# Eight PSUM banks in one list, and a limit on how far ahead weights are split

## The chip, the cores and the metric

The kernel runs on one core of a Trainium2 chip, as one program in one launch. The metric is the device time of that launch in microseconds, from several executions of the same program. Five engines work side by side, each through its own instructions in order: TensorE (PE) multiplies matrices, VectorE (DVE) and ScalarE (ACT) do elementwise work and read the matmul results, GpSimd (POOL) does a few small things, and SyncE (SP) issues nearly all DMA transfers. Engines wait for each other by semaphores.

## What is computed

Two layers, each with three sub-layers on a residual stream x of 256 tokens by 1024 features; every sub-layer is normalised and then shifted, scaled and gated by nine vectors that come from a conditioning vector c ("ada").

```python
for l in range(DEPTH):                       # 2
    mod = c_act @ ada_w[l] + ada_b[l]        # ada_w[l]: 1024 x 9216
    sh1, sc1, g1, sh2, sc2, g2, sh3, sc3, g3 = jnp.split(mod, N_MOD, axis=-1)
    h = modulate(rms_norm(x, norm_ffn1[l]), sh1, sc1)
    x = x + 0.5 * g1[:, None, :] * swiglu(h, ffn1_w_in[l], ffn1_w_out[l])   # d_ff 2816
    h = modulate(rms_norm(x, norm_mix[l]), sh2, sc2)
    x = x + g2[:, None, :] * token_mix(h, cos, sin, mix_w_in[l], sgu_w[l], sgu_b[l], mix_w_out[l])
    h = modulate(rms_norm(x, norm_ffn2[l]), sh3, sc3)
    x = x + 0.5 * g3[:, None, :] * swiglu(h, ffn2_w_in[l], ffn2_w_out[l])
return rms_norm(x, final_norm)
```

`swiglu(h, w_in, w_out)` is `(silu(g) * u) @ w_out` with `g, u` the halves of `h @ w_in`. All data are float32.

## The kernel before

**Units and splits.** Weights come from HBM in units of 512 KB, each by one DMA into one of five `raw` buffers (`NRAW`). A unit is split into a rounded part `whi` (ACT, L445) and the rest `wlo` (DVE, L446), both float32r, and a product is three matmuls: hi by hi, lo by hi and hi by lo. There are `NB` = 11 pairs of `whi`/`wlo`; a pair is used again when the matmuls of its unit are done (`ring`, `release`). `seq` is the one list of all units in order of use, with the ada units woven in between (`weave`); an ada unit is no split but one multiply-add on DVE (L430) into `aacc`.

**What sets the order.** The order on each engine is the order in which the Python code writes the instructions (a manual schedule). After each piece of work on PE the loops call `pump`, which writes the next one or two splits of `seq`, with the ada steps ahead of them, as far as the ring of 11 lets it. So ACT and DVE have splits queued for units well ahead of PE, and whatever is written after them stands behind them in the same queue.

**The feed-forward sub-layers.** There are four, called A, B (layer 0) and C, D (layer 1) here. The tokens are two halves b of 128. The first 512 columns of the hidden layer are done with the activations stationary, half by half (`ffn_gen`). The other 2304 columns go through `joint_gen`, the weight-stationary part: five chunks, J1 to J4 of 8 units and J5 of 4. A chunk keeps four accumulators (J5 two), each one PSUM bank of 128 x 512, one per 128 columns; a unit is 24 matmuls of 128x256 (L658, L660, L662), six for each accumulator. After the chunk's last unit the code writes the **evacuation**: for each accumulator a Silu on ACT (L667) and a multiply on DVE (L668), which is the last reader of the bank, and for each pair a split into `aThi`/`aTlo` (L474, L475). Then come the `pump` of that unit and the next chunk. At the end `project` multiplies by `w_out` (22 units, both halves one after the other with a lag).

**PSUM before.** Two pools: `accp` with six buffers for accumulators, and `tpp` with two for transposes and for the column sums of the ada vectors (`tp_tile`, L365, L366, L714). A pool gives its buffers out in turn, so in the joint part a chunk of four gets the two buffers that the chunk before didn't have, and then the first two that it had: its third and fourth accumulator lie where the chunk before had its first and second.

Of the kernel before, what the change touches and what calls it, by code (L numbers as in the profile page):

```python
# [23 lines left out]
NB = 11  # L24
LAG = 6
# [71 lines left out]
def trunk(ctx, tc, x_in, c_in, pos_in, ada_w, ada_b, norm_ffn1, ffn1_w_in, ffn1_w_out,  # L97
# [11 lines left out]
    accp = ctx.enter_context(tc.tile_pool(name="accp", bufs=6, space=bass.MemoryType.PSUM))  # L109
    tpp = ctx.enter_context(tc.tile_pool(name="tpp", bufs=2, space=bass.MemoryType.PSUM))  # L110
# [34 lines left out]
    def rope_tables():  # L145
# [7 lines left out]
        ang = const.tile([P, 2, 8], F32, name="ang")  # L153
# [45 lines left out]
    hThi = const.tile([P, 2, KD, P], F32R, name="hThi")  # L199
    hTlo = const.tile([P, 2, KD, P], F32R, name="hTlo")  # L200
# [102 lines left out]
    def defer(n, fn):  # L303
        pend.append([n, fn])
# [54 lines left out]
    def ada_finish(e, hi, lo, slot):  # L359
        def run():  # L360
            t = e["vec"]
            for h in range(2):
# [4 lines left out]
                V.tensor_tensor(t[:, sl], ps, t[:, sl], op=ALU.add)  # L367
            vec[(e["l"], e["kind"], e["v"] // 3 + 1)] = t
# [35 lines left out]
    def pump(quota=2, force=False):  # L404
# [3 lines left out]
        while sp[0] < len(seq) and quota > 0:  # L408
# [47 lines left out]
    wcur = [0, 0]  # L456

# [49 lines left out]
    def norm_T(b, l, i, h):  # L507
# [4 lines left out]
        for q in range(4):  # L512
# [4 lines left out]
            else:  # L517
                V.tensor_scalar(y[:, k, :], ps[:, q * P:(q + 1) * P], A, B, op0=ALU.mult, op1=ALU.add)

# [38 lines left out]
    def project(b, pi, n, operand, hook):  # L558
# [3 lines left out]
        acc = [accp.tile([P, 512], F32, name="acc", tag="acc")[:, :sl.stop - sl.start] for sl in parts]  # L562
# [12 lines left out]
        for h, sl in enumerate(parts):  # L575
# [10 lines left out]
            update(b, l, i, acc[h], sl)  # L586
            if h == 0 and SQ_D and not final:
# [13 lines left out]
    def ffn_gen(b, pi, env):  # L601
        hi, lo = hT[b]
        f = 0
        for c0, w in chunks[:1]:
            kt = 1024 // w
            acc = [accp.tile([P, 512], F32, name="acc", tag="acc") for _ in range(2)]
            for k0 in range(0, KD, kt):
                for s in range(2):
# [8 lines left out]
                    if last:  # L617
                        def ev(acc=acc, f=f, w=w):
                            a = xm[b][:, 512:1024]
                            S.activation(a[:, :w], acc[0][:, :w], AF.Silu)  # L620
                            V.tensor_tensor(a[:, :w], a[:, :w], acc[1][:, :w], op=ALU.mult)

# [66 lines left out]
    tp_ev = {}  # L689

    def tp_tile():
# [4 lines left out]
        return tpp.tile([P, 512], F32, name="tp", tag="tp")  # L696

    def evac_later(n, fn, tiles=1):
        done = []

# [4 lines left out]
        for m in range(tp_n[0] - tiles, tp_n[0]):  # L705
            tp_ev[m] = run
# [10 lines left out]
    def sgu_prep(l, env):  # L717
# [6 lines left out]
        def fin():  # L724
            ps = transposes(lambda i: wr[:, i, :], 4)
            S.activation(wT.rearrange("p g t -> p (g t)"), ps, AF.Copy)
        env["sgu_fin"] = fin
# [8 lines left out]
    def mix_gen(b, pi, env):  # L736
# [14 lines left out]
        def evac_idx():  # L751
# [4 lines left out]
            copy(D_V2, vS[:, b, 512 - VX:512], acc[:, 0:VX])  # L756
            rope(t[:, 0:320], 5, b, pool)
# [456 lines left out]
```

## Time and profile before

| | |
|---|---|
| median of three runs | 1050.22 us (1048.61 to 1052.21) |
| the profiled execution, its own time | 1047.78 us |
| its span, first to last instruction | 1046.0 us |
| PE busy | 994.6 us, 95% of the span |
| DVE, ACT busy | 780.2 us (75%), 541.6 us (52%) |
| read from HBM | 251.27 MB, mean 241 GB/s |
| chain that ended last | PE 67%, DMA 12%, DVE 12%, ACT 5%, issue 3% |

The first line is what is compared; the profile is one execution, and its span is 1.8 us shorter than its time. "Busy" of PE counts the time in which a matmul was under way, at whichever clock was granted. In the page's slices PE shows its lower digits in slices 4, 6, 16, 23 and 25 of 40 (7 to 8 tenths), all of them in the joint parts of A, B and C, and the clock row shows an 8 or a 9 beside some of them. The joint parts stand at 56 to 180 us (A), 372 to 481 (B), 565 to 688 (C) and 878 to 977 (D).

### The profile page before, as it was taken

The page shows a single profiled execution, that of the slowest core. Times are in us where ns is not written, and L with a number is a line of the kernel's source. Part 1 is how long each engine was busy: PE and PEld are TensorE (multiplying, and loading weights), DVE is VectorE, ACT ScalarE, POOL GpSimd, SP SyncE. Part 2 cuts the span into 40 slices and gives each one's busy share as a digit, 9 for nine tenths or more (in the row PEclk, how much of TensorE's full clock was granted, in tenths as well). Part 3 has the DMA queues.
Part 4 walks back from the last instruction along what each step waited for, and adds up shares of the span by engine and source line. Part 5 has one row for each costly group of instructions (what it writes and reads, how often), then busy time and mean ns, then how long its engine had stood idle before and what let it go on. Part 6 is the DMA issues. An engine that isn't in the chain of part 4 may idle for free.

```text
span 1046.0 us, 16540 instructions
## 1 busy us (share of the span) xinstructions
PE 994.6 (95%) x6352; PEld 884.1 (85%) x6352; DVE 780.2 (75%) x1095; ACT 541.6 (52%) x832; POOL 21.6 (2%) x39
## 2 busy tenths in 40 slices
PE   6996989999999998999999798999999999999997
PEld 3696979888778898998888798988888888999986
DVE  4887877778898887877668778776778878566453
ACT  5565444446577744544455444443557857444331
POOL 4000000000000000000000000000000000000000
PEclk9998999999999999999999899999999999999999
DMA  9888888985765598886848988878564548776531
GB/s 332 304 288 299 290 304 284 321 296 188 221 201 167 162 326 298 315 301 239 283 141 282 340 290 303 282 259 276 152 186 137 153 140 291 233 237 213 183 134 41
DMA packets 109774, 253.40 MB, mean 242 GB/s; under 512 B 8498, under 2 KB 26980, under 8 KB 109696
## 3 DMA queue, kind: packets, MB, share of 16 engines
q1 hardware_dynamic: 108864, 251.20, 71.7%
q8 instruction: 50, 0.82, 0.3%
q0 software_dynamic: 544, 0.63, 0.2%
q10 hardware_dynamic: 288, 0.52, 0.1%
q14 instruction: 28, 0.23, 0.1%
HBM read 251.27 MB, written 1.05 MB: 241 GB/s over the span
## 4 chain that ended last, share of the span: by engine, by line
PE 67%; DMA 12%; DVE 12%; ACT 5%; issue 3%; SPq 1%; POOL 0%; POOLq 0%; ACTq 0%; DVEq 0%
PE acc L478 14%; PE acc L480 14%; PE acc L479 13%; DMA raw<-in_ffn_w_in_dram 9%; PE acc L658 7%; PE acc L660 7%; PE acc L662 7%; DVE wlo L446 5%; ACT whi L445 3%; DVE aacc L430 3%; PE tp L714 2%; DMA raw<-in_ada_w_dram 1%; DMA sraw<-in_ada_w_dram 1%; DVE xm L668 1%; PE acc L1015 1%
## 5 line engine op out<-in xcount | busy, mean ns | idle before, releaser
L446 DVE TENSOR_TENSOR wlo<-raw,whi 128x1024 fp32r<-128x1024 f32 (+1 forms) x328 | 395.2, 1216 | 166.3 <-ACT whi L445 160.7
L445 ACT ACTIVATE whi<-raw 128x1024 fp32r<-128x1024 f32 (+1 forms) x328 | 339.0, 1048 | 301.3 <-PE acc L480 99.2
L658 PE MATMUL acc<-hThi,whi 128*128 128x256 f32 x1152 | 327.2, 284 | 29.6 <-DVE xm L668 29.6
L660 PE MATMUL acc<-hTlo,whi 128*128 128x256 f32 x1152 | 324.3, 281 | 0.0
L662 PE MATMUL acc<-hThi,wlo 128*128 128x256 f32 x1152 | 324.2, 281 | 0.0
L658 PEld LDWEIGHTS acc<-hThi,whi 128*128 128x128 f32 x1152 | 221.1, 192 | 31.3 <-DVE xm L668 31.0
L662 PEld LDWEIGHTS acc<-hThi,wlo 128*128 128x128 f32 x1152 | 221.8, 193 | 0.0
L660 PEld LDWEIGHTS acc<-hTlo,whi 128*128 128x128 f32 x1152 | 220.9, 192 | 0.3
L478 PE MATMUL acc<-whi,hThi 128*128 128x512 f32 (+1 forms) x384 | 154.7, 403 | 1.2 <-ACT hThi L1048 1.0
L480 PE MATMUL acc<-whi,hTlo 128*128 128x512 f32 (+1 forms) x384 | 148.6, 387 | 0.1
L479 PE MATMUL acc<-wlo,hThi 128*128 128x512 f32 (+1 forms) x384 | 147.5, 384 | 0.0
L430 DVE SCALAR_TENSOR_TENSOR aacc<-raw,ccol,aacc 128x1024 f32<-128x1024 f32 x112 | 143.3, 1279 | 3.0 <-DMA raw<-in_ada_w_dram 2.8
L478 PE MATMUL acc<-whi,aThi 128*128 128x512 f32 (+1 forms) x374 | 141.9, 380 | 0.0
L479 PE MATMUL acc<-wlo,aThi 128*128 128x512 f32 (+1 forms) x374 | 141.2, 378 | 0.0
L480 PE MATMUL acc<-whi,aTlo 128*128 128x512 f32 (+1 forms) x374 | 141.0, 377 | 0.0
L478 PEld LDWEIGHTS acc<-whi,hThi 128*128 128x128 f32 x384 | 72.4, 188 | 18.2 <-issue 3.2
L480 PEld LDWEIGHTS acc<-whi,hTlo 128*128 128x128 f32 x384 | 72.2, 188 | 16.0 <-DVE hTlo L1050 1.0
L479 PEld LDWEIGHTS acc<-wlo,hThi 128*128 128x128 f32 x384 | 72.4, 188 | 13.2 <-issue 0.5
L480 PEld LDWEIGHTS acc<-whi,aTlo 128*128 128x128 f32 x374 | 70.3, 188 | 13.2
L478 PEld LDWEIGHTS acc<-whi,aThi 128*128 128x128 f32 x374 | 70.4, 188 | 12.8
L479 PEld LDWEIGHTS acc<-wlo,aThi 128*128 128x128 f32 x374 | 70.4, 188 | 12.5
L491 ACT ACTIVATE xm<-x 128x512 f32<-128x512 f32 (+1 forms) x29 | 17.9, 617 | 61.7 <-DVE x L529 56.6
(152 smaller groups left out, 683.6 us busy)
## 6 DMA issues: line engine op xcount, KB each, us to landing
raw<-in_ffn_w_in_dram SPq DMA_DIRECT2D x176, 512.0 KB, 5.0
raw<-in_ada_w_dram SPq DMA_DIRECT2D x128, 512.0 KB, 5.2
raw<-in_ffn_w_out_dram SPq DMA_DIRECT2D x88, 512.0 KB, 5.0
raw<-in_mix_w_in_dram SPq DMA_DIRECT2D x40, 512.0 KB, 4.3
sraw<-in_ada_w_dram SPq DMA_DIRECT2D x32, 256.0 KB, 6.6
raw<-in_mix_w_out_dram SPq DMA_DIRECT2D x16, 512.0 KB, 3.6
vec<-in_ada_b_dram SPq DMA_DIRECT2D x6, 512.0 KB, 7.1
raw<-in_mix_w_in_dram SPq DMA_DIRECT2D x8, 324.0 KB, 3.1
```

What stands on the lines that cost most here:

```text
L430: V.scalar_tensor_tensor(aacc, e["raw"], ccol[:, j:j + 1], aacc, op0=ALU.mult, op1=ALU.add)
L445: S.activation(hi[:, :n], src, AF.Copy)
L446: V.tensor_tensor(lo[:, :n], src, hi[:, :n].bitcast(F32), op=ALU.subtract)
L478: T.matmul(ps, ahi, whi, start=first, stop=False)
L479: T.matmul(ps, ahi, wlo, start=False, stop=False)
L480: T.matmul(ps, alo, whi, start=False, stop=last)
L491: S.activation(xm[b][:, sl], x[b][:, sl], AF.Square, accum_out=ss[:, c:c + 1])
L658: T.matmul(o, wh[:, kk, sl], ahi, start=first, stop=False, skip_group_check=True)
L660: T.matmul(o, wh[:, kk, sl], alo, start=False, stop=False, skip_group_check=True)
L662: T.matmul(o, wl[:, kk, sl], ahi, start=False, stop=k == KD - 1, skip_group_check=True)
L668: V.tensor_tensor(a, a, acc[j][:, 256:], op=ALU.mult)
L714: T.transpose(ps[:, i * P:(i + 1) * P], src(i), ident)
```

## The change

1. PSUM is no longer two pools. Eight tiles of one bank each make one list, `banks`; `take()` removes the first, `give()` puts a bank at the end when the code has written its last reader. Every accumulator and every transpose tile takes from it, so each gets the bank that has been free the longest in the order of the program.
2. `pump` stops at a weight unit when `lead[0]` units are split and not yet taken by `next_w(0)`. `lead[0]` is 8 (`LEADJ`) during `joint_gen` and 11 elsewhere. What stands behind that unit in `seq`, ada units too, is held with it.
3. The small tile `ang` is allocated at another place.

No instruction of work is added or taken away. SP issues the same transfers in the same order.

```diff
@@ -106,8 +107,14 @@
-    accp = ctx.enter_context(tc.tile_pool(name="accp", bufs=6, space=bass.MemoryType.PSUM))
-    tpp = ctx.enter_context(tc.tile_pool(name="tpp", bufs=2, space=bass.MemoryType.PSUM))
+    bankp = ctx.enter_context(tc.tile_pool(name="bankp", bufs=1, space=bass.MemoryType.PSUM))
+    banks = [bankp.tile([P, 512], F32, name=f"bank{i}") for i in range(8)]
+
+    def take():
+        return banks.pop(0)
+
+    def give(*ts):
+        banks.extend(ts)
...
@@ -414,6 +422,8 @@
             r = len(ring)
+            if e["k"] == "w" and not force and len(W) - wcur[0] >= lead[0]:
+                break
             if need and r >= NB and not ring[r - NB]:
...
@@ -640,7 +655,7 @@
-            acc = [accp.tile([P, 512], F32, name="acc", tag="acc") for _ in range(nj)]
+            acc = [take() for _ in range(nj)]
...
@@ -666,6 +681,7 @@
                             S.activation(a, acc[j][:, :256], AF.Silu)
                             V.tensor_tensor(a, a, acc[j][:, 256:], op=ALU.mult)
+                            give(acc[j])
...
     def tp_tile():
...
-        return tpp.tile([P, 512], F32, name="tp", tag="tp")
+        t = tp_bank[m] = take()
+        return t
...
             if kind == "f":
                 both(n - KF)
+                lead[0] = LEADJ
                 for q, _ in enumerate(joint_gen(env)):
...
+                lead[0] = NB
             both(n)
```

ACT at the end of chunk J1 of A. `whi` of `raw` is a split, `xm0` of an accumulator is a Silu, `aThi` the split of two of them. Before:

```order
L445 ACTIVATE whi_758<-raw_679 128x1024
L445 ACTIVATE whi_767<-raw_719 128x1024
L445 ACTIVATE whi_808<-raw_756 128x1024
L445 ACTIVATE whi_817<-raw_765 128x1024
L445 ACTIVATE whi_852<-raw_806 128x1024
L445 ACTIVATE whi_863<-raw_815 128x1024
L667 ACTIVATE xm0_102<-acc_555 128x256
L667 ACTIVATE xm0_102<-acc_556 128x256
L474 ACTIVATE aThi_553<-xm0_102 128x512
```

And now, from the split of the same unit (`whi_741` here) on:

```order
L455 ACTIVATE whi_741<-raw_663 128x1024
L455 ACTIVATE whi_782<-raw_703 128x1024
L455 ACTIVATE whi_817<-raw_739 128x1024
L682 ACTIVATE xm0_107<-bank7_85 128x256
L682 ACTIVATE xm0_107<-bank1_79 128x256
L485 ACTIVATE aThi_543<-xm0_107 128x512
L682 ACTIVATE xm0_107<-bank6_84 128x256
L682 ACTIVATE xm0_107<-bank2_80 128x256
```

The evacuation moved up past three splits: the last split ahead of it was that of the tenth unit after the chunk, and is now that of the seventh.

PE at the start of J2 of A, first matmul of each accumulator. J1 had `acc_555` to `acc_558` before (`acc_918` and `acc_919` are the buffers of 555 and 556), and has banks 7, 1, 6 and 2 now. Before:

```order
L658 MATMUL acc_558<-hThi_106,whi_638 128x256
...
L658 MATMUL acc_916<-hThi_106,whi_675 128x256
...
L658 MATMUL acc_917<-hThi_106,whi_675 128x256
...
L658 MATMUL acc_918<-hThi_106,whi_675 128x256
...
L658 MATMUL acc_919<-hThi_106,whi_675 128x256
```

And now:

```order
L673 MATMUL bank2_80<-hThi_111,whi_623 128x256
...
L673 MATMUL bank5_83<-hThi_111,whi_659 128x256
...
L673 MATMUL bank0_78<-hThi_111,whi_659 128x256
...
L673 MATMUL bank3_81<-hThi_111,whi_659 128x256
...
L673 MATMUL bank4_82<-hThi_111,whi_659 128x256
```

J2 now takes no bank of J1.

PE at the start of J3 of A, where J2 had banks 5, 0, 3 and 4. `whi_1015` is an ada vector, whose column sums (`ones`) take two banks. Now:

```order
L677 MATMUL bank4_82<-hThi_111,wlo_865 128x256
L372 MATMUL bank1_79<-whi_1015,ones_97 128x512
L373 MATMUL bank1_79<-wlo_1016,ones_97 128x512
L372 MATMUL bank6_84<-whi_1015,ones_97 128x512
L373 MATMUL bank6_84<-wlo_1016,ones_97 128x512
L673 MATMUL bank2_80<-hThi_111,whi_899 128x256
...
L673 MATMUL bank7_85<-hThi_111,whi_899 128x256
...
L673 MATMUL bank5_83<-hThi_111,whi_899 128x256
...
L673 MATMUL bank0_78<-hThi_111,whi_899 128x256
```

Before, the column sums stood two units earlier, inside J2:

```order
L365 MATMUL tp_1121<-whi_979,ones_92 128x512
L366 MATMUL tp_1121<-wlo_980,ones_92 128x512
L365 MATMUL tp_1125<-whi_979,ones_92 128x512
L366 MATMUL tp_1125<-wlo_980,ones_92 128x512
L658 MATMUL acc_916<-hThi_106,whi_808 128x256
```

The sums moved to the chunk's border, and hold banks 1 and 6 when J3 takes its four: the third and fourth of J3 are the first two of J2.

## Rows read from the trace of the kernel before

**Rows 1.** Page, costliest groups: busy, mean ns of one, idle before and its releaser.

```profile
L658 PE MATMUL acc<-hThi,whi 128*128 128x256 f32 x1152 | 327.2, 284 | 29.6 <-DVE xm L668 29.6
L662 PE MATMUL acc<-hThi,wlo 128*128 128x256 f32 x1152 | 324.2, 281 | 0.0
```

**Rows 2.** Timeline, end of J1 in A: start, us, engine, line, operation, [idle before].

```profile
78.62 1.06 ACT L445 ACTIVATE whi<-raw 128x1024 fp32r<-128x1024 f32 x1 [2.57 <-DMA raw<-in_ffn_w_in_dram]
...
87.63 1.06 ACT L445 ACTIVATE whi<-raw 128x1024 fp32r<-128x1024 f32 x1 [2.81 <-DMA raw<-in_ffn_w_in_dram]
88.60 0.64 ACT L667 ACTIVATE xm<-acc 128x256 f32<-128x256 f32 x2
...
89.86 0.75 DVE L668 TENSOR_TENSOR xm<-xm,acc 128x256 f32<-128x256 f32 x2
...
90.33 0.58 PE L658 MATMUL acc<-hThi,whi 128*128 128x256 f32 x1 [9.53 <-DVE xm L668]
...
93.23 1.04 ACT L445 ACTIVATE whi<-raw 128x1024 fp32r<-128x1024 f32 x1
```

**Rows 3.** Timeline, the other waits of PE over 1 us for L668.

```profile
144.30 0.58 PE L658 MATMUL acc<-hThi,whi 128*128 128x256 f32 x1 [5.05 <-DVE xm L668]
...
399.69 0.53 PE L658 MATMUL acc<-hThi,whi 128*128 128x256 f32 x1 [3.87 <-DVE xm L668]
...
598.97 0.58 PE L658 MATMUL acc<-hThi,whi 128*128 128x256 f32 x1 [6.57 <-DVE xm L668]
...
626.25 0.39 PE L658 MATMUL acc<-hThi,whi 128*128 128x256 f32 x1 [1.71 <-DVE xm L668]
...
652.42 0.58 PE L658 MATMUL acc<-hThi,whi 128*128 128x256 f32 x1 [2.63 <-DVE xm L668]
```

**Rows 4.** Stretches behind five waits: length, PE busy (count), granted clock, DMA share, GB/s.

```profile
90.30:96.00 5.70, 5.67 (x26) 0.50 0.87 309
144.30:147.20 2.90, 2.90 (x13) 0.50 0.93 344
399.70:403.20 3.50, 3.50 (x16) 0.51 0.55 167
599.00:604.60 5.60, 5.60 (x26) 0.50 0.52 188
652.40:655.80 3.40, 3.38 (x16) 0.50 0.36 141
```

**Rows 5.** Stretches: length, busy PE, PEld, DVE, ACT, POOL, granted clock, DMA share, GB/s.

```profile
878.00:977.00 99.00, 99.00 (x872) 98.90 (x871) 65.31 (x71) 49.39 (x66) 0.00 (x0) 1.00 0.73 236
...
56.00:225.00 169.00, 154.42 (x1104) 145.82 (x1103) 134.97 (x168) 78.56 (x99) 0.00 (x0) 0.96 0.88 307
...
565.00:730.00 165.00, 152.37 (x1092) 143.90 (x1091) 126.08 (x134) 70.51 (x86) 0.00 (x0) 0.96 0.85 295
...
575.00:600.00 25.00, 17.70 (x145) 17.49 (x145) 18.88 (x20) 11.37 (x14) 0.00 (x0) 0.89 0.97 342
200.00:225.00 25.00, 25.00 (x114) 20.70 (x113) 19.46 (x17) 9.60 (x10) 0.00 (x0) 1.00 0.95 335
```

**Rows 6.** Timeline in A: split of J3's seventh unit, and the ada step behind it.

```profile
106.27 1.06 ACT L445 ACTIVATE whi<-raw 128x1024 fp32r<-128x1024 f32 x1 [1.77 <-PE acc L660]
107.36 1.23 DVE L446 TENSOR_TENSOR wlo<-raw,whi 128x1024 fp32r<-128x1024 f32 x1
108.51 1.28 DVE L430 SCALAR_TENSOR_TENSOR aacc<-raw,ccol,aacc 128x1024 f32<-128x1024 f32 x1
```

**Rows 7.** Price of a split and of an ada step on DVE, and its waits for ACT.

```profile
L446 DVE TENSOR_TENSOR wlo<-raw,whi 128x1024 fp32r<-128x1024 f32 (+1 forms) x328 | 395.2, 1216 | 166.3 <-ACT whi L445 160.7
...
L430 DVE SCALAR_TENSOR_TENSOR aacc<-raw,ccol,aacc 128x1024 f32<-128x1024 f32 x112 | 143.3, 1279 | 3.0 <-DMA raw<-in_ada_w_dram 2.8
...
119.73 1.99 ACT L445 ACTIVATE whi<-raw 128x1024 fp32r<-128x1024 f32 x2
```

More of the change, by code (lines that the diff above doesn't have):

```diff
@@ L24 @@
 NB = 11
+LEADJ = 8
 LAG = 6
@@ L367, in run @@
                 V.tensor_tensor(t[:, sl], ps, t[:, sl], op=ALU.add)
+                give(ps)
             vec[(e["l"], e["kind"], e["v"] // 3 + 1)] = t
@@ L518, in norm_T @@
                 V.tensor_scalar(y[:, k, :], ps[:, q * P:(q + 1) * P], A, B, op0=ALU.mult, op1=ALU.add)
+        give(ps)
         def split():
@@ L561, in project @@
         parts = PARTS if final and b == 1 else HALF
-        acc = [accp.tile([P, 512], F32, name="acc", tag="acc")[:, :sl.stop - sl.start] for sl in parts]
+        bk = [take() for _ in parts]
+        acc = [t[:, :sl.stop - sl.start] for t, sl in zip(bk, parts)]
         def part(k, w, h):
@@ L586, in project @@
             update(b, l, i, acc[h], sl)
+            give(bk[h])
             if h == 0 and SQ_D and not final:
@@ L605, in ffn_gen @@
             kt = 1024 // w
-            acc = [accp.tile([P, 512], F32, name="acc", tag="acc") for _ in range(2)]
+            acc = [take() for _ in range(2)]
             for k0 in range(0, KD, kt):
@@ L689, in trunk @@
     tp_ev = {}
+    tp_bank = {}
     def tp_tile():
@@ L704, in run @@
                 fn()
-        for m in range(tp_n[0] - tiles, tp_n[0]):
+                give(*[tp_bank.pop(m) for m in mine])
+        for m in mine:
             tp_ev[m] = run
@@ L726, in fin @@
             S.activation(wT.rearrange("p g t -> p (g t)"), ps, AF.Copy)
+            give(ps)
         env["sgu_fin"] = fin
@@ L756, in evac_idx @@
             copy(D_V2, vS[:, b, 512 - VX:512], acc[:, 0:VX])
+            give(acc)
             rope(t[:, 0:320], 5, b, pool)
@@ L786, in relu @@
                 S.activation(rl[:, e::2, :nk], st["lg"][e][:, :, :nk], AF.Relu)
+                give(st["lgb"][e])
             st["rl"] = rl
@@ L816, in evac_qk @@
                 S.activation(t, st["acc_k"], AF.Copy)
+            give(st["acc_" + nm])
             rope(t, 8, b, pool)
@@ L887, in evac_v @@
             copy(D_V, vS[:, b, :512 - VX], st["acc_v"][:, :512 - VX])
+            give(st["acc_v"])
         def pv(g):
@@ L891, in pv @@
             if g == 0:
-                st["pv"] = accp.tile([P, 512], F32, name="acc", tag="acc")
+                st["pv"] = take()
             ps = st["pv"]
@@ L904, in evac_att @@
             split_T(st["pv"].rearrange("p (k t) -> p k t", k=4), nhi[:, 4:8, :], nlo[:, 4:8, :])
+            give(st["pv"])
         def evac_gelu(nm):
@@ L908, in evac_gelu @@
             S.activation(t, st["acc_" + nm], AF.Gelu)
+            give(st["acc_" + nm])
             st[nm] = t
@@ L912, in sgu_mm @@
             va = st["va"]
-            ps = accp.tile([P, 512], F32, name="acc", tag="acc")
+            ps = take()
             for g in range(4):
@@ L924, in sgu_out @@
                                        op0=ALU.add, op1=ALU.mult)
+            give(ps)
         def tr_a():
@@ L973, in mix_gen @@
         for nm, c0, w in MIX_CHUNKS:
-            acc = accp.tile([P, 512], F32, name="acc", tag="acc")
+            acc = take()
             for k0 in range(0, KD, 2):
@@ L1025, in start_acc @@
         n_sd[0] += KD // SJ
+        if g + 2 >= NG:
+            give(su["dps"][g % 2])
     def start_col(g):
@@ L1057, in start_x @@
             S.activation(su["xhT"][:, h * 4:h * 4 + 4, b, :], ps.rearrange("p (k t) -> p k t", k=4), AF.Copy)
+            give(ps)
     def load_cols(l):
@@ L1070, in col_T @@
         S.activation(cols[:, l, :], ps[:, :96], AF.Copy)
+        give(ps)
     rope_it = rope_tables()
@@ L1081, in start @@
         su["acc"] = aap.tile([P, D], F32, name="aacc", tag="aacc")
-        su["dps"] = [accp.tile([P, 512], F32, name="acc", tag="acc") for _ in range(2)]
+        su["dps"] = [take() for _ in range(2)]
         dma_fill()
```

15 lines of the change are left out of this document (12 added, 3 removed).

## The prediction

> **What bounds the kernel now.** I read the page's engine shares first (the table above): PE is busy 994.6 of 1046 us, so the kernel can only win where PE stands still or runs slowly. Then the costliest groups, for PE's idle time: nearly all of it in the joint parts stands before L658, 29.6 us, and is ended by DVE's multiply L668, the last reader of an accumulator; before L662, the first to need `wlo`, it is 0.0 [rows 1]. So in the joint parts PE waits for banks and never for weights.
>
> The timeline says why. J1 of A has ended and PE has started J2, when it reaches J2's third accumulator, which lies where J1 had its first. It stands there for 9.53 us, until 90.33 [rows 2], so from 80.80. J1's evacuation was ready to go, but its Silu stood on ACT behind the split of the tenth unit after the chunk, which itself waited 2.81 us for its transfer and began at 87.63; the Silus came at 88.60, the multiplies at 89.86 [rows 2]. The split three places earlier began at 78.62 [rows 2]. The other waits are 5.05 us in A, 3.87 in B, and 6.57, 1.71 and 2.63 in C [rows 3]: with the first, 29.4 of the 29.6 us. D has none.
>
> What a wait costs is more than its length: behind five of the six PE runs at a granted clock of 0.50 (1.2 instead of 2.4 GHz) for 5.7, 2.9, 3.5, 5.6 and 3.4 us, though busy all the time [rows 4]. Half of that, 10.5 us, is lost. Through all of D, where PE never stops, the clock is 1.00 [rows 5]. D also gives the pace: 872 matmuls in 99.00 us, 0.1135 us each, so 2.72 us for a unit of 24 and 21.8 us for a chunk of eight.
>
> **The change, part by part.**
>
> *Banks by longest free.* At the border J1 to J2 in A the new order gives J2 four banks that J1 didn't have, so the wait has nothing to wait for, and J1's evacuation has a whole chunk of 21.8 us. The waits removed: A 9.53 + 5.05 = 14.58, B 3.87, C 10.91, together 29.4 us. With them goes half of the slow stretches behind them: A (5.7 + 2.9)/2 = 4.3, B 1.75, C 4.5, together 10.5. At most, then: A 18.9, B 5.6, C 15.4, in sum 39.9 us.
>
> *What isn't removed.* J3 of A still takes two banks of J2, as its third and fourth accumulators, since the column sums hold two others. After J2's end PE has 12 matmuls (1.4 us) to do before it wants the first of them, and ahead of those four of twice the width, some 0.9 us by D's pace: 2.3 us of grace. J2 would now run from 79.4 (80.80 less those 1.4) to 101.2, so PE is there at 103.5. J2's Silu stands behind the split of J3's seventh unit, which began at 106.27, and waited 1.77 us of that for PE, which will now be earlier [rows 6]: from 104.5, then. After it come its `wlo` of 1.23 us and an ada step of 1.28 ahead of the multiply on DVE [rows 6], whose single cost is 0.75/2 = 0.38 [rows 2]. As timed now the bank is free at 109.8 + 0.4 = 110.2, and without the 1.77 at 108.4: a new wait of 6.7 or of 4.9 us. The lower bound is zero, if ACT gets there before J2 ends. As one evacuation no longer sits between those splits and the transfers have some room left, I take 4.4, near the upper rows. With half of a slow stretch like the 2.9 us that followed the 5.05 us wait [rows 4] it is 5.9 (bounds 0 to 8.2).
>
> B's last border has the same pattern, with the fourth accumulator only: 18 matmuls, 2.0 us, before it is wanted, so a wait shorter than the 3.87 there now is possible. I leave B at 5.6 and keep 2.6 for the range. The 1.71 us wait shows that a short one costs no clock.
>
> *The transposes of `aacc`* and the column sums move two to four units later, the same instructions on the same engines. Their readers are two to three units away, and I cost it at nothing; covered by that distance, the price without cover is one border wait of some 2 us.
>
> *The cap of eight.* Splits that stood ahead of the evacuation now stand behind it. It removes no work. In A the evacuation takes ACT from 88.60 to 93.23, 4.6 us [rows 2], and splits written behind it come that much later; their cover is the stock, 8 x 2.72 = 21.8 us of PE's work. I cost it at nothing while that holds, and its failing is the third rival.
>
> *Supply.* A faster PE wants its weights sooner. The DMA share is 0.88 over 56 to 225 us and 0.85 over 565 to 730, where the best stretches of 25 us show 0.95 and 0.97 [rows 5]. With 0.96 as the ceiling A's 169 us can shrink to 154.9, C's 165 to 146.1: gains up to 14.1 and 18.9. So 18.9 in A is more than the transfers allow, 18.9 - 5.9 = 13.0 is just within, and 15.4 in C is near it. In 575 to 600, where C's longest wait lies, the transfers are already at the ceiling [rows 5]. For this closeness I take 1.5 off each; this is a choice between 0 and what the first rival would take.
>
> Sum: A 18.9 - 5.9 - 1.5 = 11.5; B 5.6; C 15.4 - 1.5 = 13.9; together 31.0 us. The profiled execution took 1047.8, which makes 1016.8; the median of the runs shown is 2.4 higher, 1050.2, which makes 1019.2. I say 1018.
>
> The clock term stands on [rows 4]: slow stretches only behind waits of 2.6 us and more. The Trainium skill (TensorE: Matmul & The Clock Gate, "A second HAM failure mode: psum-queue depth-cycling") speaks against part of it: it tells of a kernel that cycled through PSUM banks and whose clock fell again and again from micro-idling between groups of matmuls. By that page the 10.5 us would stay and the new time would be about 1027. D in this trace cycles through its six buffers at a clock of 1.00, so the trace doesn't agree.
>
> **The rivals.**
>
> *Supply takes over (first rival).* PE loses the wait for the bank and soon waits for `whi` or `wlo` instead. For it: the split at 93.23 is that of the eleventh unit after J1, the one at 119.73 that of the eighteenth [rows 2, 7]: seven units (and one ada vector) in 26.5 us, while PE at full pace takes 19.0. DVE waits 160.7 us in all for `whi` [rows 7], so it can't run ahead of ACT. Against it: even at today's times the eighteenth unit would be split by about 122, and PE without its first wait would want it at 79.4 + 17 x 2.72 = 125.6, later still with the new wait. If it decides, the long first waits of A and C don't come back; there stays in A 5.05 + 1.45 - 5.9 = 0.6, in B 5.6, in C 1.71 + 2.63 + 1.7 = 6.0: a gain of 12.2, 1036 to 1038.
>
> *Only the releaser changes (second rival).* The same limit everywhere, or the new waits as long as the old: 1047.8 for the execution, 1050 for the median. The rows speak against it, since the waits before L662 are 0.0 and D's DMA share of 0.73 [rows 5] shows that the same loop is not limited by transfers. The Trainium skill (the same page, "HAM oscillation — how this bites in real kernels") has such a case: a kernel which double-buffered PSUM gained nothing more, 126.6 us against 125.5. No wait for PSUM like those of [rows 3] is told of there.
>
> *The stock of eight runs dry (third rival, slower).* With eight instead of eleven units in stock, a burst of evacuation on ACT and ada steps on DVE can outlast it. On DVE eight units take 8 x 1.22, in A some seven ada steps 7 x 1.28 [rows 7], four multiplies (1.5) and two splits of `aT` of about 0.6 (an estimate from half a `wlo`): 21.4 us, and with 0.5 us of waiting for ACT at each split (160.7/328) [rows 7] 25.3. That is above PE's 21.8 for a chunk, so a stock shrinks by 3.5 us a chunk and would be gone after six; A has four and a half. It decides from about 27 us for eight units, where the 21.8 us are gone by the end of A. Then PE waits 4 to 5 us at each late border of A and C, now with the clock loss, and no wait for a bank is left to give the stock time to refill: four times 5, and the waits that stay, some 10 us above today: 1060.
>
> **How the numbers follow.** Forecast 0.70 (1007 to 1026: the gain of 31 with A's new wait at 0 and nothing for supply is 39.9, 1008 to 1010; with that wait at 8.2, B at 2.6 and 3 off A and C each, 23 to 24, 1024 to 1026). Supply takes over 0.20 (1027 to 1042 around 1036). Only the releaser changes 0.05 (1050). Stock runs dry 0.05 (1060). Eight in ten: the forecast with half of the first rival, 1006 to 1036. About 0.3%, 3 us, is what a measurement of this kernel can tell from no change: faster 0.90, the first two cases; same 0.05; slower 0.05.
>
> **What would show it.** In the profile after, the idle time before the first matmul of a unit ended by the multiply falls from 29.6 to under 8 us, with one wait at the start of J3 in A. The joint parts fall from 124 to about 112 us (A), 109 to 103 (B) and 123 to 109 (C), and D stays at 99. The granted clock is 1.00 in B and C, and the DMA share over A rises to about 0.94. The first rival would show PE's idle time behind the splits (L455, L456), the second the same sum with other names, the third a longer A. Wrong I would be above all if the supply in A, at 0.88 of 0.96, gives out late in the joint part or in the `project` behind it.

## The result, and the profile after

The changed kernel took 1038.74 us (median of four, 1037.3 to 1041.44) against 1050.06: a ratio of 0.9894, interval 0.9867 to 0.9921. A second measurement gave 0.9928 (0.9903 to 0.9952). It is faster by 8 to 11 us. The forecast was 31, and 1038.7 lies outside the range, whose upper end was 1036.

The waits went as forecast. The page of the changed kernel, costliest groups (busy, mean ns of one, idle before and its releaser), for [rows 1] and [rows 7]:

```profile
L456 DVE TENSOR_TENSOR wlo<-raw,whi 128x1024 fp32r<-128x1024 f32 (+1 forms) x328 | 394.0, 1215 | 121.0 <-ACT whi L455 119.0
...
L673 PE MATMUL bank<-hThi,whi 128*128 128x256 f32 x1152 | 327.6, 284 | 4.2 <-DVE xm L683 4.2
...
L677 PE MATMUL bank<-hThi,wlo 128*128 128x256 f32 x1152 | 323.6, 281 | 0.0
```

The idle time before an accumulator's first matmul fell from 29.6 to 4.2 us, all of it one wait; 1.37 us more stand before a transpose at 138 us, which waits for a bank from the same multiply (L683). The timeline of the changed kernel at the end of J1 in A, on ACT, which answers [rows 2], and PE at the start of J3:

```profile
79.54 1.06 ACT L455 ACTIVATE whi<-raw 128x1024 fp32r<-128x1024 f32 x1 [2.82 <-DVE aacc L440]
80.51 0.64 ACT L682 ACTIVATE xm<-bank 128x256 f32<-128x256 f32 x2
...
111.21 0.58 PE L673 MATMUL bank<-hThi,whi 128*128 128x256 f32 x1 [4.22 <-DVE xm L683]
```

The Silu comes at 80.51 instead of 88.60, behind the split that begins at 79.54. The wait of 4.22 us at the start of J3 is the one that the prediction had put at 4.4.

Where the other 20 us went is seen when the joint parts and what lies between them are set out. From the start of a part's first joint matmul to the start of its last, and the time between the parts, in us, by the two profiled executions (spans 1046.0 and 1035.4):

| | before | after | change |
|---|---|---|---|
| up to A | 56.5 | 57.6 | +1.1 |
| A | 122.8 | 113.2 | -9.6 |
| A to B | 192.7 | 199.7 | +7.0 |
| B | 108.6 | 104.8 | -3.8 |
| B to C | 85.1 | 86.1 | +1.0 |
| C | 121.6 | 106.4 | -15.2 |
| C to D | 191.1 | 195.0 | +3.9 |
| D | 98.4 | 103.4 | +5.0 |
| behind D | 69.2 | 69.2 | 0 |

Two things stand out. D had no wait to lose and is 5.0 us longer. And 7.0 us of A's 9.6 and 3.9 of C's 15.2 come back behind the joint parts.

Stretches of the changed kernel (length, busy PE, PEld, DVE, ACT, POOL, granted clock, DMA share, GB/s), for [rows 5]: joint part A, then D, then three stretches of 10 us in A:

```profile
57.00:171.00 114.00, 108.41 (x900) 107.66 (x899) 93.57 (x128) 56.68 (x76) 0.00 (x0) 0.99 0.87 304
...
863.00:966.50 103.50, 103.50 (x871) 103.45 (x870) 61.28 (x68) 45.48 (x62) 0.00 (x0) 1.00 0.61 213
...
80.00:90.00 10.00, 10.00 (x88) 10.00 (x87) 7.90 (x14) 5.80 (x10) 0.00 (x0) 1.00 0.72 246
110.00:120.00 10.00, 8.79 (x63) 8.79 (x64) 8.58 (x15) 5.13 (x11) 0.00 (x0) 0.83 0.63 218
140.00:150.00 10.00, 10.00 (x87) 10.00 (x87) 9.01 (x11) 4.54 (x5) 0.00 (x0) 1.00 0.65 208
```

D: 871 matmuls in 103.50 us, where before it was 872 in 99.00 [rows 5], at the same granted clock of 1.00 and with PE busy all the time. The matmuls follow each other more slowly; no view of waits shows that. Read from start to start (over all joint matmuls of D that start less than 160 ns after the one before), the pace is 119.1 ns on average instead of 113.4. In A, B and C the averages went from 115.3, 114.8 and 116.0 to 118.3, 118.7 and 119.1: times 864 matmuls each, 2.6, 3.4, 2.7 and in D 4.9 us, 13.6 in all.

A: the DMA share is 0.87, not the 0.94 that was forecast. Over the joint part alone it was 0.87 before, too; the 0.88 of [rows 5] is taken over a longer stretch. In the changed kernel it falls to 0.72, 0.63 and 0.65 in the three stretches shown. The kernel before has such dips at other places. Its joint part A and two stretches of 5 us:

```profile
56.00:180.00 124.00, 109.42 (x903) 108.58 (x902) 99.39 (x134) 60.10 (x79) 0.00 (x0) 0.94 0.87 300
...
120.00:125.00 5.00, 5.00 (x46) 5.00 (x45) 4.28 (x7) 2.99 (x5) 0.00 (x0) 1.00 0.56 175
145.00:150.00 5.00, 5.00 (x36) 5.00 (x36) 4.03 (x7) 3.32 (x6) 0.00 (x0) 0.78 0.48 182
```

In both kernels a dip comes with an evacuation. While DVE works on that, it finishes no split and so frees no `raw` buffer, and SP issues no transfer of weights: in the changed kernel none between 83.09 and 88.67.

```profile
83.09 0.37 SPq L350 DMA_DIRECT2D raw<-in_ffn_w_in_dram  x1
88.67 0.34 SPq L362 DMA_DIRECT2D raw<-in_ada_w_dram  x1
...
82.97 0.75 DVE L683 TENSOR_TENSOR xm<-xm,bank 128x256 f32<-128x256 f32 x2
87.42 1.23 DVE L456 TENSOR_TENSOR wlo<-raw,whi 128x1024 fp32r<-128x1024 f32 x1
```

And the wait behind A's joint part, PE at the column sums of an ada vector, with ACT there:

```profile
191.06 0.51 PE L372 MATMUL bank<-whi,ones 128*128 128x512 f32 x1 [3.33 <-ACT whi L455]
192.32 0.60 PE L373 MATMUL bank<-wlo,ones 128*128 128x512 f32 x1 [0.76 <-DVE wlo L456]
...
189.95 1.06 ACT L455 ACTIVATE whi<-aacc 128x1024 fp32r<-128x1024 f32 x1 [3.78 <-DVE aacc L440]
```

PE waits for the split of `aacc`, ACT for the last ada step (L440). In the kernel before that split began at 191.3, in the changed one at 189.95: PE had left the joint part 8.5 us earlier, the stream of units was 1.4 us earlier.

### The profile page after: what moved, and what is told of

It is laid out like the page before. It is cut to its first block, busy times and chain, and to the rows that moved or that the text cites. A ratio compares the mean times of both kernels' runs of the same rounds, so it can differ in the third digit from the quotient of the medians.

```text
span 1035.4 us, 16480 instructions
## 1 busy us (share of the span) xinstructions
PE 1000.1 (97%) x6352; PEld 889.5 (86%) x6352; DVE 780.2 (75%) x1095; ACT 540.4 (52%) x832; POOL 20.1 (2%) x39
## 4 chain that ended last, share of the span: by engine, by line
PE 61%; DVE 15%; DMA 14%; ACT 6%; issue 4%; SPq 0%; POOL 0%; POOLq 0%; ACTq 0%; DVEq 0%
PE bank L489 12%; PE bank L491 12%; PE bank L490 12%; PE bank L673 7%; PE bank L675 7%; PE bank L677 7%; DMA raw<-in_ffn_w_in_dram 5%; DVE wlo L456 5%; DMA raw<-in_ada_w_dram 4%; DVE aacc L440 3%; ACT whi L455 3%; DMA raw<-in_ffn_w_out_dram 2%; PE bank L734 2%; DMA sraw<-in_ada_w_dram 1%; DVE xm L683 1%
## 5 line engine op out<-in xcount | busy, mean ns | idle before, releaser
L673 PE MATMUL bank<-hThi,whi 128*128 128x256 f32 x1152 | 327.6, 284 | 4.2 <-DVE xm L683 4.2
L675 PE MATMUL bank<-hTlo,whi 128*128 128x256 f32 x1152 | 324.5, 282 | 0.0
L677 PE MATMUL bank<-hThi,wlo 128*128 128x256 f32 x1152 | 323.6, 281 | 0.0
L673 PEld LDWEIGHTS bank<-hThi,whi 128*128 128x128 f32 x1152 | 217.1, 188 | 4.8 <-DVE xm L683 4.4
L675 PEld LDWEIGHTS bank<-hTlo,whi 128*128 128x128 f32 x1152 | 217.6, 189 | 0.3
L677 PEld LDWEIGHTS bank<-hThi,wlo 128*128 128x128 f32 x1152 | 217.6, 189 | 0.0
L489 PE MATMUL bank<-whi,hThi 128*128 128x512 f32 (+1 forms) x384 | 154.8, 403 | 1.1 <-ACT hThi L1084 1.0
L491 PE MATMUL bank<-whi,hTlo 128*128 128x512 f32 (+1 forms) x384 | 148.1, 386 | 0.2
L490 PE MATMUL bank<-wlo,hThi 128*128 128x512 f32 (+1 forms) x384 | 148.3, 386 | 0.0
L440 DVE SCALAR_TENSOR_TENSOR aacc<-raw,ccol,aacc 128x1024 f32<-128x1024 f32 x112 | 143.3, 1279 | 4.4 <-DMA raw<-in_ada_w_dram 4.2
L489 PE MATMUL bank<-whi,aThi 128*128 128x512 f32 (+1 forms) x374 | 142.6, 381 | 0.0
L502 ACT ACTIVATE xm<-x 128x512 f32<-128x512 f32 (+1 forms) x29 | 17.9, 617 | 62.3 <-DVE x L541 56.6
```

What stands on the lines that cost most here:

```text
L440: V.scalar_tensor_tensor(aacc, e["raw"], ccol[:, j:j + 1], aacc, op0=ALU.mult, op1=ALU.add)
L489: T.matmul(ps, ahi, whi, start=first, stop=False)
L490: T.matmul(ps, ahi, wlo, start=False, stop=False)
L491: T.matmul(ps, alo, whi, start=False, stop=last)
L502: S.activation(xm[b][:, sl], x[b][:, sl], AF.Square, accum_out=ss[:, c:c + 1])
L673: T.matmul(o, wh[:, kk, sl], ahi, start=first, stop=False, skip_group_check=True)
```

## The experiments

Times are medians; the ratio to the kernel before on the same chip stands with its interval. "A to B" in this section is from the start of joint part A to the start of B: 315.6 us before, 312.9 and 313.5 in two profiles of the changed kernel. It comes from one profiled execution each.

### The tile that moved

`ang` has 64 bytes in each partition. Before, it was allocated behind `hThi` and `hTlo`, the two moving operands of the joint part; now it lies between them. By the order of allocation `hTlo` begins at byte 44800 instead of 44736, and nothing else that the joint part reads has another address; the traces don't show addresses.

```diff
     hThi = const.tile([P, 2, KD, P], F32R, name="hThi")
-    ang = const.tile([P, 2, 8], F32, name="ang")
     hTlo = const.tile([P, 2, KD, P], F32R, name="hTlo")
...
+        ang = const.tile([P, 2, 8], F32, name="ang")
         for b in range(2):
             V.tensor_scalar(ang[:, b, :], invt, posf[:, b:b + 1], None, op0=ALU.mult)
```

> The changed kernel with one edit undone: the 64-byte tile ang is allocated last again, so that hTlo, the second moving operand of the joint part, lies 64 bytes lower, at 44736 instead of 44800, as before the change. Theory 1 (the missing gain went into the pace of the joint matmuls, 117.8 to 119.3 ns from start to start instead of 113.3, and the address of hTlo is the cause): the joint part D falls from 103.5 to about 98.6 us, all joint pieces together win some 13 us, and the time is about 1025. Rival (the pace comes from the banks or the order of the evacuation): D stays at 103.5 and the time at 1038.

The mirror image, the kernel before with `ang` moved and nothing else:

> The kernel before with only ang moved between hThi and hTlo, nothing else. Theory 1 (address of hTlo): D goes from 98.6 to 103.5 us and the joint matmuls there from 113.3 to about 119 ns; the time rises by 10 to 18 us, to 1060 to 1068. Rival: 1050, D at 98.6.

Measured: 1033.18 us, 0.9876 (0.9836 to 0.9915), and 1052.18 us, 1.0063 (1.0039 to 1.0086). D in the changed kernel with `ang` back, and then in the kernel before with `ang` moved:

```profile
863.00:962.00 99.00, 99.00 (x873) 98.87 (x872) 61.79 (x68) 45.70 (x63) 0.00 (x0) 1.00 0.65 223
```

```profile
881.00:984.50 103.50, 103.50 (x870) 103.45 (x869) 64.52 (x71) 49.23 (x64) 0.00 (x0) 1.00 0.70 227
```

The pace follows the address in both directions: 98.4 us with `hTlo` at 44736, 103.4 at 44800, whichever pools and cap go with it. The change of pools has no part in it. On the whole time the effects were smaller than those in the joint parts: 1025 had been expected of the first, and 10 to 18 us of the second, which lost 6.3 by the medians. To have its worth in the changed kernel, both were measured again side by side:

> The changed kernel once more, to stand beside the next one on the same chip. 0.989 of the time before.

> The changed kernel with hTlo at its old address, once more. By the joint parts alone (pace of 113.4 to 114.9 instead of 118.3 to 119.1 ns) it wins 9.5 us on the changed kernel. If the stream of transfers sets the end of A, and of C, it gets back only what B and D win, 3.3 and 5.0 us, and loses some to waits for ada vectors behind the joint parts: 4 to 6 us.

1040.36 and 1032.36 us, 0.9928 (0.9903 to 0.9952) and 0.9858 (0.9830 to 0.9887): the 64 bytes cost 8.0 us, more than the 4 to 6 that were expected. The intervals do not touch.

What about the address counts? Four more placements, one run and one profile each, all on the kernel before:

> The kernel before with ang ahead of hThi, so that both moving operands lie 64 bytes higher: hThi at 36608, hTlo at 44800, both multiples of 128, where before both were 64 over one. Nothing else moves. Read in D, where no wait disturbs the pace. If what counts is that the two operands stand alike (both 64 over, or both on a multiple): D at 98.4 us and 113.4 ns. If a start 64 over is what is fast for each: D above 103.4. If a multiple of 128 is what is fast: D below 98.4.

> The kernel before with hThi at 36608, a multiple of 128, and hTlo at 44864, 64 over one; the weights' buffers lie 128 bytes higher. If the two operands have to stand alike, D is as slow as in the changed kernel, about 103.4 us; if hTlo's own place is what counts, 98.4.

> The kernel before with both moving operands on multiples of 128, as in the slow run with both aligned, and with the weights' buffers whi, wlo and raw moved by 64 bytes too, so that these now start 64 over a multiple of 128. If what counts is how the moving operand lies against the weights: D back from 104.1 to 98.4 us. If the place of the moving operand itself counts (64 over): D stays at 104.1.

> The kernel before with both moving operands 32 bytes higher, 96 over a multiple of 128, weights on a multiple of 128 as before. If only the halves of 128 bytes count, each operand beginning in the upper half: D 98.4. If the start has to be at 64: D at 102 to 104.

The four runs took 1056.26, 1054.73, 1052.89 and 1062.95 us. D, and the mean pace in each part, by the starts of `hThi`, `hTlo` and of the weights, each as bytes over a multiple of 128 (the first row is the kernel before, the second the one with `ang` moved):

| hThi | hTlo | weights | D, us | pace in D, ns | pace in A, B, C, ns |
|---|---|---|---|---|---|
| 64 | 64 | 0 | 98.4 | 113.4 | 115.3, 114.8, 116.0 |
| 64 | 0 | 0 | 103.4 | 119.1 | 118.2, 118.8, 118.8 |
| 0 | 64 | 0 | 102.4 | 118.0 | 120.3, 119.4, 120.2 |
| 0 | 0 | 0 | 104.1 | 120.0 | 119.9, 119.9, 119.9 |
| 96 | 96 | 0 | 104.1 | 120.0 | 120.0, 119.9, 119.9 |
| 0 | 0 | 64 | 101.9 | 117.4 | 115.0, 114.5, 113.7 |

These runs were planned to be read in D, and for the last row D misleads. The kernel before has two paces, 113.3 and 117.8 ns (see the last section), and D is the one part in which it stays at the first. With the weights moved the paces are the same two: mostly 113.3 to 113.9 ns in B and C, and 117.8 in D from 890 us on, behind a transpose at 888. Stretches of 10 us in C and one in D, first with the weights moved, then with both operands at 0 and the weights not moved; the count of matmuls behind PE's busy time is what to compare:

```profile
610.00:620.00 10.00, 10.00 (x90) 10.00 (x89) 8.54 (x10) 3.86 (x5) 0.00 (x0) 1.00 0.95 319
640.00:650.00 10.00, 10.00 (x91) 10.00 (x90) 8.43 (x9) 3.19 (x3) 0.00 (x0) 1.00 1.00 347
950.00:960.00 10.00, 10.00 (x88) 10.00 (x87) 6.90 (x7) 5.26 (x6) 0.00 (x0) 1.00 0.62 216
```

```profile
610.00:620.00 10.00, 10.00 (x86) 10.00 (x85) 9.19 (x11) 3.78 (x4) 0.00 (x0) 1.00 0.95 320
640.00:650.00 10.00, 10.00 (x86) 10.00 (x85) 9.36 (x10) 3.22 (x4) 0.00 (x0) 1.00 1.00 352
950.00:960.00 10.00, 10.00 (x86) 10.00 (x85) 7.68 (x11) 5.28 (x8) 0.00 (x0) 1.00 0.50 155
```

So moving the weights gives the paces of the kernel before back, and the place of the operands against the weights fits all six rows: 113.3 and 117.8 ns where both stand 64 bytes apart from them, 120.0 where neither does, in between where one does. The operand's own place alone doesn't fit the last row, and standing alike is not enough. These are single profiles; why the place counts isn't shown, and operands and weights all at 64 weren't tried.

### Cap and list, one at a time

With `ang` back, the list without the cap (`LEADJ = 11`), and the two pools with the cap:

> The list of eight banks with ang last again and LEADJ 11 instead of 8, so that the evacuation stands behind the split of the tenth unit after the chunk again. Theory 2 (the cap costs supply: with three units less in stock the ada vectors come late, and PE waits 3.3 us for the column sums at 188 us and 2.2 and 1.5 us for transposes at 672 and 700): those waits vanish, and the time is some 5 us below that of the kernel with the cap. Rival (the cap is needed to bring the evacuation to ACT in time): the wait at the start of J3 in A grows from 4.2 to 7 us and more, others come at B's last border, and the time is some 5 us above it.

> The kernel before, two pools of six and two, with only the cap of eight. If the cap is what removes the waits, the Silu at the end of J1 in A comes at about 80 instead of 88.6, the waits of 29.4 us shrink to 1 to 2 us at each border, no slow clock follows them, and the time is 1025 to 1032. If the list is what removes them, the time stays above 1042 with waits of 3 us and more at the borders.

Measured: 1042.34 us, 0.9970 (0.9947 to 0.9992), and 1033.83 us, 0.9864 (0.9817 to 0.9910). List and cap together, on the same chip, took 1033.18. So with five raw buffers the cap is what won, and the list by itself won under 6 us; theory 2, by which the kernel without the cap was to be 5 us faster, falls. Without the cap three waits for accumulators stay, 19.6 us in all: the list alone removes a third of the 29.6. In the pools with the cap the Silu at the end of J1 in A comes at 80.16, but five waits stay, 12.0 us in all and up to 5.15, not 1 to 2 us at a border as expected, and the time is 2 us above the forecast. The list with the cap has one such wait of 4.77 us, and yet no better time. The list without the cap, at the border J3 to J4 of A, PE and ACT:

```profile
143.58 0.58 PE L673 MATMUL bank<-hThi,whi 128*128 128x256 f32 x1 [9.28 <-DVE xm L683]
...
135.74 1.06 ACT L455 ACTIVATE whi<-raw 128x1024 fp32r<-128x1024 f32 x1 [2.60 <-DMA raw<-in_ffn_w_in_dram]
138.24 1.06 ACT L455 ACTIVATE whi<-raw 128x1024 fp32r<-128x1024 f32 x1 [1.45 <-DMA raw<-in_ffn_w_in_dram]
140.88 1.06 ACT L455 ACTIVATE whi<-raw 128x1024 fp32r<-128x1024 f32 x1 [1.58 <-DMA raw<-in_ffn_w_in_dram]
141.84 0.64 ACT L682 ACTIVATE xm<-bank 128x256 f32<-128x256 f32 x2
```

The evacuation stands behind three splits, and each of those waits for its transfer. It is late not because splits take long but because their weights have not landed. The wait for column sums at 190 us is gone in this kernel, as theory 2 had it, but others came, and A to B takes 314.4 us.

A cap of nine:

> As the one with ang back, with a cap of nine instead of eight. The evacuation stands one split later on ACT, some 3 us. If the cap costs transfers (the DMA share falls to 0.64 in 80 to 90, 110 to 120 and 140 to 150 us while the cap holds the splits) the column sums at 190 us come a little earlier, and the wait at J3 of A grows from 4.8 to 7 us; about 1033 to 1036, the same within the measurement. If supply in A doesn't depend on the cap: 1036 to 1038.

1032.11 us, 0.9846 (0.9819 to 0.9874), the same as eight within the measurement. The wait for column sums at 190 us shrank to 0.5 us, one of 6.43 us came at J3's end instead, and A to B took 312.3 us. Wherever the waits lie, the sum from A to B is nearly the same.

### Why A gives its gain back

> As the one with ang back, but one ada vector of eight transfers (4 MB) is moved from A to the token mix behind it (VA1 5 to 4, VA2 1 to 2), where the DMA share is 0.55 to 0.75. Theory 3 (from A's start to B's start the stream of transfers is the limit, so that whatever A's joint part wins is given back in the waits for column sums at 190 us): A's transfers end some 12 us earlier, the wait of 5.8 us at 186 to 192 and the slow clock behind it vanish, and B starts 7 to 10 us earlier, at 362 to 365 instead of 371.8: 1023 to 1026. Rival (the wait is a matter of order on ACT and DVE, not of transfers, or the mix has no room): B starts where it did, 1033.

1033.93 us, 0.9869 (0.9843 to 0.9894), against 1032.36 with the vector in place: no gain. Half of theory 3 held: the joint part A fell to 104.2 us, and the last weights of the projection were split 9 to 12 us earlier. But B started at 371.0 as before. The steps and transfers that were moved made PE wait in the mix:

```profile
243.53 0.59 PE L734 MATMUL bank<-ident,idx 128*128 128x128 f32 x3 [0.73 <-DVE idx L702]
252.49 0.72 PE L803 MATMUL bank<-kiT,qiT 64*128 64x128 f32 x8 [2.87 <-ACT kiT L791]
257.24 0.63 PE L734 MATMUL bank<-ident,row 128*128 128x128 f32 x4 [1.07 <-DVE row L702]
```

Next, less DVE work with the same transfers, and fewer transfers. Both kernels leave out part of the sums of ada vectors. The edit of the first:

```diff
-                    V.scalar_tensor_tensor(aacc, e["raw"], ccol[:, j:j + 1], aacc,
+                    wd = 128 if e["l"] == 0 and e["v"] in (2, 3, 4, 5, 7) else D
+                    V.scalar_tensor_tensor(aacc[:, :wd], e["raw"][:, :wd], ccol[:, j:j + 1], aacc[:, :wd],
```

> The changed kernel with ang back, and the 35 multiply-adds of the five ada vectors in A done on 128 of 1024 columns (the rest of the sum is left out): some 35 us less work of DVE in A, with all transfers as they are. If the transfers are the limit from A's start to B's start: no gain there beyond 3 us, 1029 to 1032. If DVE's chain of splits and steps is the limit: B starts 8 us or more earlier, 1024 or less.

> The changed kernel with ang back, and six of the eight transfers of the last ada vector of A left out, with their steps (that vector's sum is incomplete). At 1.55 us each, the time of 512 KB at 340 GB/s, the transfers end 9 us earlier. If the transfers are the limit up to B's start, B starts 7 to 9 us earlier than the 372 us with ang back, and the time is 1023 to 1026. If the limit in A is something else, or the time goes into waits in the mix as when the vector was moved there: less than 3 us.

1025.47 us, 0.9761 (0.9728 to 0.9794), and 1027.05 us, 0.9776 (0.9750 to 0.9801): both win, neither as one theory alone would have it. A to B takes 310.0 and 312.4 us, against 315.1 and 316.2 in two profiles with only `ang` back. Cutting 35 us of DVE work gave 5 to 6 of them; leaving out six transfers (9 us by the estimate above) and their steps gave 3 to 4, no more than the cap of nine with all its work. The rest of the gain lies behind B or in the spread between executions. Neither the engine nor the transfers seem to be the limit by themselves. What links them is the raw buffer: a transfer can't start before DVE has finished with a buffer, and a split can't start before the transfer has landed. In the changed kernel SP waits for `wlo` before weight transfers 207 times, 428.9 us in all, and ACT waits 160.7 us for feed-forward weights to land. With five buffers each waits for the other.

So: seven buffers instead of five, all work as it was. The room comes from one pair of `whi`/`wlo` less, which asks for a lag of five between the halves in the projections; the control has these two edits and five buffers.

```diff
-NB = 11
+NB = 10
...
-LAG = 6
-NRAW = 5
+LAG = 5
+NRAW = 7
```

> The changed kernel with ang back, with seven raw buffers instead of five, paid for by ten pairs of whi and wlo instead of eleven (and a lag of five instead of six between the halves in the projections, which ten pairs need). If the stretches in which the cap holds the splits and the DMA share falls to 0.64 are what limits the stream in A: two more transfers run in each of them, some 3 us each, the dips shrink, and from A's start to B's start it takes 308 to 311 us instead of 315 to 316; the time is 3 to 8 us under the control with five. If DVE's chain of splits and steps is the limit, no difference.

> The control for the run with seven raw buffers: ten pairs of whi and wlo, lag of five, five raw buffers. About the time of the kernel with ang back, 1032 to 1036.

1009.75 us, 0.9648 (0.9603 to 0.9693), against 1038.74 us, 0.9919 (0.9897 to 0.9941) for the control: 29 us by two buffers, where 3 to 8 had been expected. (The control's own two edits cost some 4 to 6 us beside the kernel with only `ang` back, by the ratios; no cost had been expected.) A to B takes 300.0 us instead of 317.9, and C to D 296.9 instead of 305.9. ACT's waits for feed-forward weights fall from 173.2 us to 60.6. The stretches from 57 to 161 us and at 140 with seven buffers, and then from 58 to 171 and at 140 in the control:

```profile
57.00:161.00 104.00, 103.58 (x896) 102.90 (x895) 93.51 (x130) 57.35 (x78) 0.00 (x0) 1.00 0.93 336
...
140.00:150.00 10.00, 10.00 (x87) 10.00 (x86) 9.93 (x12) 4.37 (x5) 0.00 (x0) 1.00 1.00 373
```

```profile
58.00:171.00 113.00, 105.55 (x896) 104.52 (x895) 91.01 (x127) 56.20 (x76) 0.00 (x0) 0.97 0.87 300
...
140.00:150.00 10.00, 10.00 (x89) 10.00 (x88) 9.04 (x11) 4.84 (x7) 0.00 (x0) 1.00 0.65 203
```

The share over A rises from 0.87 to 0.93, and one of the three dips is gone; the other two are shallower (0.77 for 0.71 at 80, 0.71 for 0.67 at 110). At the end of J1 with seven buffers, on ACT:

```profile
79.19 0.38 ACT L682 ACTIVATE xm<-bank 128x256 f32<-128x256 f32 x1 [0.30 <-PE bank L677]
80.06 0.63 ACT L485 ACTIVATE aThi<-xm 128x512 fp32r<-128x512 f32 x1 [0.49 <-DVE xm L683]
```

ACT stands ready and waits for PE: the eight splits are done before the chunk ends. The page's line of L673 shows no idle time at all, even at J3 of A:

```profile
L673 PE MATMUL bank<-hThi,whi 128*128 128x256 f32 x1152 | 321.1, 279 | 0.0
```

Last, what list and cap are worth once the stream has room:

> The kernel before, two pools and no cap, with seven raw buffers, ten pairs and a lag of five. If the late evacuation came only from splits that waited for transfers: the waits for banks vanish here too, and the time is 1010 to 1016, so that the list and the cap are worth nothing beside two buffers. If the place of the evacuation behind nine or ten splits counts by itself: waits of 4 us and more stay at the borders, with slow clocks behind them, and the time is 1030 to 1040.

> The list of eight banks with ang back and seven raw buffers, ten pairs, lag of five, but a cap of ten, which is no cap. With the cap it took 1009.8. If the list alone is enough once the stream has room: 1010 to 1014. If the cap is still needed for the borders where a chunk lands on banks just left (J3 of A, J4 of B): one or two waits of 4 us and more, 1016 to 1026.

1020.37 us, 0.9721 (0.9666 to 0.9775), with the two pools and no cap, and 1019.54 us, 0.9716 (0.9670 to 0.9761), with the list and no cap. In each kernel A alone still waits for banks; first the pools' earlier wait, then the list's only one:

```profile
83.58 0.58 PE L658 MATMUL acc<-hThi,whi 128*128 128x256 f32 x1 [2.33 <-DVE xm L668]
```

```profile
132.88 0.58 PE L673 MATMUL bank<-hThi,whi 128*128 128x256 f32 x1 [6.28 <-DVE xm L683]
```

In the pools a second of 4.21 us follows, at 135 us. So of the 29.6 us of waits in [rows 1] 23.1 went without list and cap, and the splits that had no data are the likely cause. It isn't shown for the two buffers by themselves: with one pair less, one split fewer can stand ahead of the evacuation, and pools with ten pairs and five buffers weren't tried. The pools' time lies between its two forecasts, the list's is where its second theory had it. List without cap shows no gain beside pools without cap (intervals overlap). With the cap on top, the list wins 7 us more by the ratios, 10 by the medians of the two series: its one wait of 6.28 us, and half of the 3.2 us that PE then runs at a clock of 0.50, make 7.9, and the joint part A is 7.8 shorter. Pools with the cap and seven buffers weren't tried. The list with the cap, `ang` back and seven buffers, at 1009.75 us, beats both kernels of this study.

## Why the prediction was wrong

**Right: the waits and what they cost.** That PE stood for banks and not for weights, that the Silu was late behind a split that waited for its transfer, and that the list and the cap together would remove all but one wait, is what the changed kernel shows: 29.6 to 4.2 us, 4.22 at J3 of A for 4.4. The clock term came back too: the granted clock is 1.00 in B, C and D, and only the 4.22 us wait has a slow stretch in a joint part. The rule that was weighed in the prediction, from the Trainium skill (TensorE: Matmul & The Clock Gate, "A second HAM failure mode: psum-queue depth-cycling"), has no support here: with eight banks in rotation D runs at 1.00 from end to end.

**Wrong: which edit removes the waits.** The prediction gave them to the list ("the wait has nothing to wait for") and priced the cap at nothing. With five buffers the list alone left 19.6 of the 29.6 us and won under 6 us; the cap alone, on the two pools, took 1033.83 us, where list and cap together took 1033.18. The prediction priced both together, so this didn't shift its sum.

**Wrong: an edit was left out of the sum.** The prediction has no term for `ang`. The section on the change names it as the third part, and it was passed over as a small tile at another place. It moved an operand that 1152 of the 3456 joint matmuls read, and all three kinds became slower; the forecast that "D stays at 99" fell with it: 103.4. This cost 8.0 us, measured side by side, of the 20 to 23 us that were missing. No row of the trace of before could give the price; that the address of a moving operand in the hottest loop had changed could be read from the order of allocation, and should have stood in the sum as an unknown with bounds on both sides.

**Wrong in size: the supply.** Beside `ang`, this is the step that failed, and the larger one. The sum took "1.5 off each" in A and C, "a choice between 0 and what the first rival would take", and left the time between the joint parts as it was. The kernel with `ang` back shows the term by itself: against the kernel before, its joint parts are 33.1 us shorter (10.3 in A, 7.0 in B, 15.8 in C), where 31.0 had been forecast, and the stretches between them are 17.9 us longer (9.8 from A to B, 2.3 from B to C, 5.8 from C to D). So some 18 us came back there, where the sum had 3 for supply. In the changed kernel, of A's 9.6 us, 7.0 came back behind the joint part: 4.1 in the two waits at the column sums, 1.7 in the half clock behind them, 0.7 in a longer wait of the mix. Of C's 15.2, 3.9 came back, 3.7 of them in two waits for the transposes of an ada vector (2.18 and 1.50 us, at 674 and 701). The mechanism is the first rival's, with one difference: PE doesn't wait for `whi` or `wlo` of weights in the joint part, where after the first few units it has four or more in stock, but behind it, for the ada vectors, which are woven between the weights and have no stock.

The term was that small because of the ceiling. The gain in A was bounded by raising the DMA share from 0.88 to 0.96, as if only the bandwidth were in the way. But with five buffers the transfers depend on when DVE releases one, and during each evacuation it releases none, with the cap or without. Over the same 56 to 225 us the share went from 0.88 to 0.89, and over the joint part it stayed at 0.87; with seven buffers it is 0.93. The split that waits 2.81 us for its transfer [rows 2] didn't tell this, for at 80 to 90 us the share was 0.93. The dips would have: 0.56 and 0.48 in the stretches of 5 us above, right behind evacuations.

**The rivals.** The first, at 1036 to 1038 us with a chance of 0.20, named the measured time, but by a coincidence of two causes: without the 64 bytes the change gives 1032 to 1033. In the second the releaser was to change everywhere; it did so in part. The third didn't come: stock fell in A to five units, some 13 us, and in C to four, never to nothing. The range ended at the near edge of the first rival, which had held a fifth of the chance; with the unknown of `ang` in it, it would have reached further. The low end of the forecast's own gains adds up to 22.7 us and not 23 to 24, which would have made its range reach to about 1027.

## What to carry to other kernels

Every edit in a diff needs a term, also the one that seems to be housekeeping: here 64 bytes in front of a matmul operand cost 8 us of 1040. When a wait at a border is ended by an evacuation that stands behind weight splits, ask first why those splits are late; if they wait for transfers while the transfer engines have gaps, landing buffers come first: two more were worth 29 us here, list and cap together 13 to 15 with five. And a gain in one part is only kept if the stream that feeds the next parts can run ahead too: look at the start-to-start time of the parts, which from A to B stayed at 310 to 319 us in every kernel with five buffers, was 309 to 310 with seven and no cap, and fell to 300 with seven, list and cap.

## What the runs showed of the hardware

The pace of joint matmuls (128x256, float32r) depends on where the moving operands start against the weights, at the same granted clock of 1.00. With both 64 bytes apart from them (over multiples of 128) it is 113.3 or 117.8 ns, with both 0 or both 96 bytes apart 120.0, and with one of them 64 bytes apart it changes between values from 117.8 to 121.2. The kernel before shows the two paces of one placement: over 10 us the mean is 113.3 ns in most stretches and 117.8 in others (among them 136 to 165 us in A, 407 to 438 in B, 663 to 687 in C), and each change from one to the other lies right behind transposes or column sums that came between the joint matmuls, or behind a stretch at half clock. What sets it wasn't tried.
